# A hybrid decoder step on one core: memory attention with its queries computed by token chunks over all heads, square sums of four heads at once, TensorE's order written by hand, and four output projection tiles placed among the last attention units

## The chip, the core and the metric

The program runs on one core of a Trainium2 chip. The core has TensorE (matmuls into PSUM), VectorE (DVE), ScalarE (ACT), GpSimd (POOL), and SyncE (SP), whose queue issues nearly all of this kernel's transfers. The metric is the device time of one execution in microseconds (us). The kernel before was run three times: median 1817.87 us, from 1817.65 to 1817.94.

## The reference

One layer of a decoder trunk for 1024 prompt tokens and 32 sample tokens (8 sequences of 4), 1056 tokens in all, width 1024, in fp32. Three residual sub-layers follow each other: a mixer (chunked gMLP beside latent attention, then an output projection), a cross-attention into 256 memory tokens, and a gated ConvFFN. The change touches the second:

```python
def mem_attend(h, mk, mv, w_mq, g_mq, w_mo):          # h = rms_norm(x, g_mem_x)
    q = rms_norm((h @ w_mq).reshape(n, t, MEM_HEADS, MEM_HEAD_DIM), g_mq)   # 4 heads of 128
    s = einsum('nthd,nmhd->nhtm', q, mk) * MEM_HEAD_DIM ** -0.5
    p = softmax(s)
    o = einsum('nhtm,nmhd->nthd', p, mv).reshape(n, t, MEM_WIDTH)
    return o @ w_mo
```

The prompt's 1024 tokens share one memory (`mk`, `mv` computed earlier in the same program). Each of the 8 sample sequences has its own cached keys and values of 256 memory tokens, read from DRAM. The result is added to `x`, and the sum goes to the ConvFFN.

## The kernel before

Every fp32 operand of a large matmul is split into a high and a low part of a faster type (`split`, L197: ACT writes the high part, DVE the low part), and a product is three matmuls, high by high, high by low, low by high (`mm3`, L180). Activations lie transposed, features on partitions and tokens along the free axis.

Memory attention (`mem_attention`, L1804) comes behind the mixer's output projection (tile `b`, operands `mx`). Its work is in units of one head `h` and a group `g` of 256 prompt tokens, 16 units in all.

- `query(h, c)` projects head `h` for chunk `c` of three (384, 384 and 288 tokens; the last 32 are the sample tokens): 24 matmuls into PSUM tile `b`. ACT squares the result (`qsq`) and casts it (`qh`), DVE makes `ql`. `tok_sums` (L292) then sums the squares over the 128 features: three matmuls against a column of ones, one column of output each, into tile `st`. After the third chunk DVE works out the head's norm factors `rm` in a chain of small instructions.
- `scores(h, g)`: 12 matmuls into `s` and the softmax (DVE maximum, ACT exponential, DVE division).
- `values(h, g)`: four transposes of the probabilities into `t`, the split into `th` and `tl`, 6 matmuls with the values into `t`, and the split back into `qh`, `ql`.
- The sample part: `sample_scores` and `sample_values` go through the 8 sequences, each with one 512 KB tile of keys or values in `skT` (6 buffers, and once a buffer of `raw`).

Loops before: over heads, in each over the three chunks; the units of head `h - 1` stand between the chunks of head `h`; the units of head 3 and the sample part stand alone behind the last query. The projection with `w_mo` follows (`out`, L2002: per tile 24 matmuls into `y`, 16 tiles for two token halves of 528), then the FFN.

A head's projection weight is brought in by `stream` (L1566): a 512 KB load into `raw` (3 buffers), POOL multiplies it by the gain in place (L1576), ACT casts it to `hi` (L201), DVE makes `lo` (L202). `hi` and `lo` have 3 buffers each. The memory's own keys and values pass through `raw` as well (`memory`, L1822).

What sets the order: the functions write the program, and a list scheduler then orders the instructions of every engine and of the SP queue by its own estimates, unless the code stands under `manual_schedule` for an engine. In this stage nothing did before. Each engine, and SP, then runs its list strictly in that order, and a row waits until all it needs is there, with everything behind it on that engine.

## Time and profile before

| what | us |
|---|---|
| median of three runs | 1817.87 |
| the profiled execution's own time | 1818.09 |
| its span, first to last instruction | 1816.4 |
| TensorE busy in the span | 1794.4 (99%) |
| mean granted TensorE clock | 0.997 of full |
| first query matmul of memory attention | at 981.65 |
| first matmul of the `w_mo` projection | at 1083.02 |
| first matmul of the FFN's block that follows the projection | at 1135.99 |

Times "at" are microseconds from the start of the span. A timeline row gives start, duration, engine, line, operation, tile written and tiles read, shape, and behind it, in brackets, how long the engine had been idle and who released it. The durations of neighbouring matmuls overlap, so the cost of one is the distance from its start to the next start. `st<-ones,qsq` is a sum of squares; `b<-xh,hi` a query matmul; `y<-qh,hi` the projection.

### The profile page before, as it was taken

How to read it: one execution, taken by the hardware profiler on the slowest of the kernel's cores; microseconds unless marked ns; L12 is line 12 of the kernel's file. 1: busy time of each engine (PE TensorE's matmuls, PEld its weight loads, DVE VectorE, ACT ScalarE, POOL GpSimd, SP SyncE). 2: the span in 40 equal slices, each digit the busy share in tenths (PEclk: the TensorE clock that was granted, in tenths of full speed). 3: DMA queues.
4: the chain of work that ended last, by engine and by line, in shares of the span. 5: the costliest groups of instructions: out<-in, count | busy, mean ns of one | idle time of the engine just before them, and what ended most of it. 6: DMA issues, size and time to landing. Idle time of an engine off the chain costs nothing.

```text
span 1816.4 us, 39284 instructions
## 1 busy us (share of the span) xinstructions
PE 1794.4 (99%) x14194; PEld 1702.2 (94%) x14194; DVE 1354.0 (75%) x2796; ACT 918.5 (51%) x1909; POOL 713.5 (39%) x868
## 2 busy tenths in 40 slices
PE   9999999999999999999999999999999999999999
PEld 8999777769999999998899979999999999999999
DVE  7864777657678777787645768998888888878664
ACT  7435676766556565556433557533333333344442
POOL 1021655534455454553023012476667777400000
PEclk9999999999999999999999999999999999999999
DMA  8101354558776666663645156223222222595252
GB/s 325 47 18 67 119 178 128 164 174 233 223 205 188 192 188 181 186 192 124 190 153 190 37 188 213 64 81 94 74 71 73 81 72 93 145 324 163 87 148 78
DMA packets 153188, 261.19 MB, mean 144 GB/s; under 512 B 20897, under 2 KB 97538, under 8 KB 152994
## 3 DMA queue, kind: packets, MB, share of 16 engines
q1 hardware_dynamic: 152130, 257.63, 46.0%
q8 instruction: 112, 1.84, 0.4%
q10 hardware_dynamic: 864, 1.05, 0.2%
q14 instruction: 82, 0.67, 0.1%
HBM read 212.79 MB, written 45.82 MB: 142 GB/s over the span
## 4 chain that ended last, share of the span: by engine, by line
PE 81%; DVE 5%; ACT 1%; issue 1%; POOL 1%; SPq 0%; DMA 0%; DVEq 0%; ACTq 0%; POOLq 0%
PE s L186 22%; PE d L186 12%; PE b L186 8%; PE F L186 7%; PE X L186 7%; PE E L186 7%; PE A L186 3%; PE y L186 3%; PE o L1047 2%; PE o L1538 2%; PE tp L1032 1%; PE tp L186 1%; PE s L1423 1%; PE tp L985 1%; PE t L186 1%
## 5 line engine op out<-in xcount | busy, mean ns | idle before, releaser
L186 PE MATMUL s<-w2h,ch 128*128 128x256 f32 x1018 | 301.8, 297 | 0.0
L186 PE MATMUL s<-w2h,cl 128*128 128x256 f32 x1018 | 293.3, 288 | 0.0
L186 PE MATMUL s<-w2l,ch 128*128 128x256 f32 x1018 | 292.9, 288 | 0.0
L186 PEld LDWEIGHTS s<-w2h,ch 128*128 128x128 f32 x1018 | 191.5, 188 | 3.3 <-issue 2.9
L186 PEld LDWEIGHTS s<-w2h,cl 128*128 128x128 f32 x1018 | 191.3, 188 | 0.4 <-DVE rqa L258 0.4
L186 PEld LDWEIGHTS s<-w2l,ch 128*128 128x128 f32 x1018 | 191.7, 188 | 0.0
L1459 DVE TENSOR_REDUCE ss<-sq 128x16 f32<-128x1024 f32 x128 | 155.3, 1213 | 29.2 <-ACT sq L1456 29.1
L1408 POOL TENSOR_TENSOR cl<-cT,ch 128x512 fp32r<-128x512 f32 x64 | 86.1, 1346 | 196.7 <-ACT ch L1404 184.2
L1456 ACT ACTIVATE sq<-s 128x512 f32<-128x512 f32 x128 | 76.5, 598 | 72.4 <-PE s L186 72.2
L201 ACT CAST a<-brb 128x528 fp32r<-128x528 f32 x77 | 48.8, 634 | 109.3 <-PE d L186 105.9
L1453 ACT ACTIVATE sq<-s 128x512 f32<-128x512 f32 x128 | 76.8, 600 | 49.8 <-PE s L186 38.2
L202 DVE TENSOR_TENSOR a<-brb,a 128x528 fp32r<-128x528 f32 x77 | 54.3, 708 | 55.1 <-ACT a L201 55.0
L186 PE MATMUL d<-a,w 128*128 128x264 f32 x768 | 95.2, 284 | 0.0
L186 PEld LDWEIGHTS d<-a,w 128*128 128x128 f32 x768 | 94.3, 188 | 0.0
L2148 POOL TENSOR_TENSOR lo<-s,hi 128x1024 fp32r<-128x1024 f32 x20 | 63.3, 3164 | 45.9 <-ACT hi L2147 45.9
L186 PE MATMUL mm<-wlo,xh 128*128 128x256 f32 (+3 forms) x272 | 77.0, 286 | 0.1
L2203 ACT COPY a<-A 128x264 f32<-128x264 f32 x43 | 16.1, 376 | 120.6 <-PE A L186 113.2
L186 PE MATMUL mm<-whi,xh 128*128 128x256 f32 (+3 forms) x272 | 77.0, 285 | 0.0
L186 PE MATMUL mm<-whi,xl 128*128 128x256 f32 (+3 forms) x272 | 76.9, 287 | 0.0
L1404 ACT CAST ch<-cT 128x512 fp32r<-128x512 f32 x128 | 73.5, 628 | 0.2 <-issue 0.2
L2269 POOL TENSOR_TENSOR cv<-cv,row 128x1056 f32<-128x1056 f32 x22 | 65.1, 2958 | 21.0 <-ACT cv L2268 21.0
L186 PE MATMUL d<-a,hi 128*128 128x264 f32 x552 | 72.0, 284 | 0.0
(756 smaller groups left out, 6359.3 us busy)
## 6 DMA issues: line engine op xcount, KB each, us to landing
cT<-cT SPq DMA_DIRECT2D x256, 160.0 KB, 2.6
ck<-ck SPq DMA_DIRECT2D x256, 144.0 KB, 3.5
raw<-w_up SPq DMA_DIRECT2D x44, 512.0 KB, 3.6
wsumd<-wsum SPq DMA_DIRECT2D x26, 512.0 KB, 3.9
actd<-cv SPq DMA_DIRECT2D x44, 264.0 KB, 2.3
brb<-actd SPq DMA_DIRECT2D x44, 264.0 KB, 5.9
wsum<-w_down SPq DMA_DIRECT2D x22, 512.0 KB, 3.6
raw<-wsumd SPq DMA_DIRECT2D x20, 512.0 KB, 3.8
```

What stands on the lines that cost most here:

```text
L186: x = self.nc.tensor.matmul(out, l, r, start=first and i == 0, stop=last and i == len(seq) - 1)
L201: first = {"act": nc.scalar.copy, "pool": nc.gpsimd.tensor_copy, "dve": nc.vector.tensor_copy}[eng](hi, src)
L202: low = lambda: nc.vector.tensor_tensor(lo, src, hi, ALU.subtract)
L1047: nc.tensor.matmul(u["o"][g : g + 64, o : o + m * P], s["v"][:, j, h % 4], th[:, z * P : (z + m) * P], start=j == 0, stop=b == len(banks) - 1,
L1404: nc.scalar.copy(d["h"][:, k], src[k])
L1408: (nc.vector if k else nc.gpsimd).tensor_tensor(d["l"][:, k], src[k], d["h"][:, k], ALU.subtract)
L1453: nc.scalar.activation(sq[:, 0], ps[:, :, n0 : n0 + 256], AF.Square)
L1456: nc.scalar.activation(sq[:, 1], pt.rearrange("p (e d) -> p e d", e=2), AF.Square)
L1459: yield lambda: nc.vector.tensor_reduce(s["ss"][:, g0 : g0 + 2].rearrange("p e (z h) -> p z e h", z=2), sq.rearrange("p z e (h d) -> p z e ...
L1538: nc.tensor.matmul(s["o"][j * 32 : j * 32 + 32], S[:, q * 4 + j], d["ck"][:, j, :257], start=q == 0 and j > 0, stop=q == 7)
L2148: eng.tensor_tensor(lo, src, hi, ALU.subtract)
L2269: nc.gpsimd.tensor_tensor(cv, cv, row, ALU.mult)
```

## The change

Queries now run by token chunk, and inside a chunk over the four heads: `query(h, c)` with four chunks of 256, 256, 256 and 288 tokens, 16 calls of 24 matmuls. All four projection weights are thus used in the first four calls and again in each later chunk; the fourth weight has buffers of its own (`wx`), the others keep the three of `hi` and `lo` until the last chunk.

The sums of squares of the four heads of a chunk are made together: `square_sums(c)` multiplies a block of 32 columns of ones with each head's 256 or 288 squares, one head per 32 output partitions, ACT copies the result (`rows`), and `roots(c)` transposes it (two transposes, three for the last chunk) so that tokens come to lie on partitions; one DVE chain then serves four heads.

TensorE's order is written by hand as 23 slots: in slot `s` stand the scores of unit `s - 5`, the query of number `s`, the values of unit `s - 7` and the transposes of unit `s - 6`. The slots from 16 on have no query; the sample part and four projection tiles (`ahead`, first token half, output columns of `j` = 0 and 1) stand there. Those four tiles take their PSUM from the query's `b`, their residual from early loads, and their result lies in the room of FFN operands that are written later (`room`). `out` does the other twelve. `skT` has 5 buffers now and no tile in `raw`; the sample keys' first five loads are written in the program behind slot 7. The other engines and the SP queue are still ordered by the scheduler.

```diff
-    def stream(self, src, kt, g=None, eng="act", tag="", raw=None):
+    def stream(self, src, kt, g=None, eng="act", tag="", raw=None, hl=None):
 
         nc = self.nc
         p, pr = (self.wd, self.wd) if tag else (self.wp, self.wr)
         if raw is None:
             raw = self.t(pr, [P, 8, P], F32, "raw" + tag)[:, :kt]
             nc.sync.dma_start(raw, src)
-        hi, lo = (self.t(p, [P, 8, P], FR, x + tag)[:, :kt] for x in ("hi", "lo"))
+        hi, lo = hl or (self.t(p, [P, 8, P], FR, x + tag)[:, :kt] for x in ("hi", "lo"))
...
-        roots = self.t(pp, [P, 512], F32, "sx", 1)
+        bank = lambda tag, n: self.t(pp, [P, 512], F32, tag, n)
+        for tag in "bst":
+            bank(tag, 2)
...
+        wx = [self.t(p, [P, 8, P], FR, f"wx{n}") for n in "hl"]
...
-        w, st = {}, {}
+        w, qsq, pr, ts = {}, {}, {}, {}
 
         def query(h, c):
-            o, n = CH[c]
-            if c == 0:
-                st[h] = self.t(pp, [P, 512], F32, "st", 1)
-            ps = self.t(pp, [P, 512], F32, "b", 2)[:, :n]
+            o, n = 256 * c, 288 if c == 3 else 256
+            ps = bank("b", 2)[:, :n]
             self.mm3(ps, [(w[h][0][:, k], w[h][1][:, k]) for k in range(8)], [(xh[:, k, o : o + n], xl[:, k, o : o + n]) for k in range(8)])
-            sq = self.t(p, [P, 384], F32, "qsq", 2)
-            nc.scalar.activation(sq[:, :n], ps, AF.Square)
-            self.pad(sq, c)
+            qsq[h] = self.t(p, [P, 288], F32, f"qsq{h}", 1)[:, :n]
+            nc.scalar.activation(qsq[h], ps, AF.Square)
             self.split(qh[:, h, o : o + n], ql[:, h, o : o + n], ps, gmq)
-            self.tok_sums(st[h], sq, c, self.ones)
-            if c < 2:
-                return
-            nc.vector.tensor_scalar(qs[:, h], ps[:, 256:], gmq, None, ALU.mult)
-
-            r = rm[:, h]
-            nc.vector.tensor_tensor(r, st[h][:, :9], r3, ALU.mult)
-            nc.vector.tensor_tensor(r, r, r3, ALU.mult)
-            self.rsqrt(p, r, r, 1.0 / 128)
-            nc.vector.tensor_tensor(r, r, r3, ALU.mult)
-
-        pr = {}
-
-        def scores(h, g):
-            ps = self.t(pp, [P, 512], F32, "s", 2).rearrange("p (e n) -> p e n", e=2)
+            if c == 3:
+                nc.vector.tensor_scalar(qs[:, h], ps[:, 256:], gmq, None, ALU.mult)
+                nc.gpsimd.tensor_tensor(qm[h], blk, qs[:, h].unsqueeze(1).broadcast_to([P, NB, NS]), ALU.mult)
...
+        rows = self.t(p, [P, 384], F32, "rows", 1)
+
+        def square_sums(c):
+
+            n = 288 if c == 3 else 256
+            st = bank("st", 1)[:, :n]
+            for h in range(4):
+                nc.tensor.matmul(st[32 * h : 32 * h + 32], self.ones[:, :32], qsq[h], start=True, stop=True)
+            if c == 3:
+                nc.gpsimd.memset(rows[:, n:], 1.0)
+            nc.scalar.copy(rows[:, :n], st)
+
+        def roots(c):
+
+            m, t = 3 if c == 3 else 2, slice(2 * c, 9 if c == 3 else 2 * c + 2)
+            st = bank("st", 1)[:, : m * P].rearrange("p (k n) -> p k n", k=m)
+            for k in range(m):
+                nc.tensor.transpose(st[:, k], rows[:, k * P : k * P + P], self.ident)
+            x = self.t(p, [P, 3, 4], F32, "rsq", 2)[:, :m]
+            r = rt[:, t].unsqueeze(2).broadcast_to([P, m, 4])
+            nc.vector.tensor_tensor(x, st.rearrange("p k (h e) -> p k h e", h=4)[:, :, :, 0], r, ALU.mult)
+            nc.vector.tensor_tensor(x, x, r, ALU.mult)
+            xf = x.rearrange("p k h -> p (k h)")
+            self.rsqrt(p, xf, xf, 1.0 / 128)
+            nc.vector.tensor_tensor(rm[:, t], x, r, ALU.mult)
...
+        units = [(h, g) for g in range(4) for h in range(4)]
+
+        def scores(i):
...
+        def trans(i):
+            src = pr.pop(i)
+            tp = bank("t", 2).rearrange("p (k n) -> p k n", k=2)
             for k in range(2):
                 for e in range(2):
                     nc.tensor.transpose(tp[:, k, e * P : e * P + P], src[:, e, k * P : k * P + P], self.ident)
-            th, tl = (self.t(p, [P, 2, 256], FR, x, 2) for x in ("th", "tl"))
-            self.split(th, tl, tp)
+            ts[i] = [self.t(p, [P, 2, 256], FR, x, 1) for x in ("th", "tl")]
+            self.split(*ts[i], tp)
+
+        def values(i):
+            h, g = units[i]
...
+                    skv.append(self.t(ps_, [P, 4, 256], F32, "skT", 5))
...
+        def sample_scores(b0, b1):
+            if b0 == 0:
+                sample["s"] = bank("sx", 1)[:, :256]
+            for b in range(b0, b1):
                 kT = skv.pop(0)
                 for h in range(4):
-                    nc.tensor.matmul(sample["s"][heads[h]], sample["q", h][:, b], kT[:, h], start=b == 0, stop=b == NB - 1)
-                if b != 6:
-                    sample_load(1)
-            if z:
-                sample["p"] = self.t(ps_, [P, 1, 256], F32, "pf")
-                self.softmax(ps_, sample["p"], sample["s"].unsqueeze(1), P, sample["sc"])
-
-        def sample_values():
-            tp = self.t(pp, [P, 512], F32, "st", 1)[:, :256].rearrange("p (k n) -> p k n", k=2)
+                    nc.tensor.matmul(sample["s"][heads[h]], qm[h][:, b], kT[:, h], start=b == 0, stop=b == NB - 1)
+                sample_load(1)
...
+        def sample_trans():
...
+                if b < 4:
+                    f()
+                else:
+                    sample["m", b] = f
...
+                if b0 == 0:
+                    sample_load(1)
+                    sample["m", b + 4]()
...
-        for h in range(4):
-            w[h] = self.stream(I["w_mq"][h], 8, "g_mem_x")
-            if h == 2:
-                sample_load(6)
+        def project(h):
+            hl = None if h < 3 else wx
+            w[h] = self.stream(I["w_mq"][h], 8, "g_mem_x", hl=hl)
+
+        def slot(s):
+            c, h = divmod(s, 4)
+            if s >= 5:
+                scores(s - 5)
+            query(h, c)
+            if c and h == 0:
+                roots(c - 1)
+            if s >= 7:
+                values(s - 7)
+            if s >= 6:
+                trans(s - 6)
             if h == 3:
-                sample_load(1, self.t(self.wr, [P, 8, P], F32, "raw").rearrange("p k n -> p (k n)").rearrange("p (h n) -> p h n", h=4))
-            for c in range(3):
-                query(h, c)
-                if h == 0 and c == 0:
-                    self.token_roots(p, roots, r3, 2)
+                square_sums(c)
...
+        with tc.manual_schedule(engines={E.PE}):
+            for s in range(16):
+                if s < 4:
+                    project(s)
+                slot(s)
+                if s == 0:
+                    self.token_roots(p, bank("sx", 1), r3, 2)
+                    nc.vector.tensor_copy(rt, r3)
                     memory()
+                if s == 7:
+                    sample_load(5)
+            self.close("x")
+            px = self.open("xo1", side="right")
+            flat = lambda x: x.bitcast(F32).rearrange("p k n -> p (k n)").rearrange("p (j n) -> p j n", j=2)
+            room = [flat(self.t(px, [P, 4, QT], FR, f"{n}1{q}")) for n in self.FORMS[:3] for q in "hl"]
+            y0 = [room[:2], room[2:4]]
...
+            early = {(j, e): residual(pe, 0, 4 * e + j) for j in range(2) for e in range(2)}
+            wo = [weight(j) for j in range(3)]
+
+            def ahead(j, e):
+
+                res = early[j, e]
+                for c in range(2):
+                    t = slice(c * QT, c * QT + QT)
+                    ps = bank("b", 2)[:, :QT]
+                    self.mm3(ps, [(wo[j][0][:, 4 * e + k], wo[j][1][:, 4 * e + k]) for k in range(4)], [(qh[:, k, t], ql[:, k, t]) for k in range(4)])
+                    nc.vector.tensor_tensor(res[:, t], ps, res[:, t], ALU.add)
+                leave(pe, 0, j, e, res, y0[0])
+
+            for s in range(16, 23):
+                if s < 21:
+                    scores(s - 5)
+                if s < 19:
+                    sample_scores(3 * (s - 16), min(3 * (s - 15), NB))
+                elif s < 22:
+                    ahead(*divmod(s - 19, 2))
+                if s == 16:
+                    roots(3)
+                if s == 19:
+                    sample_trans()
+                if s > 20:
+                    sample_values(4 * (s - 21))
+                if s == 22:
+                    ahead(1, 1)
+                values(s - 7)
+                if s < 22:
+                    trans(s - 6)
+            sample_out()
...
-        for j in range(4):
-            if j == 3:
-                w[j] = weight(j)
-            out(0, j, w[j], y1[j // 2])
-            if j % 2:
-                self.operands(y1[j // 2], j // 2, ops[0], self.FORMS)
-        w[0] = weight(0)
+        self.operands(y0[0], 0, ops[0], self.FORMS)
+        wo.append(weight(3))
+        for j in (2, 3):
+            out(0, j, wo[j], y0[1])
+        self.operands(y0[1], 1, ops[0], self.FORMS)
+        for n in self.FORMS[:3]:
+            form(self.pools["xo1"][1], 1, n)
+        wo[0] = weight(0)
```

How the orders move, at three places. The names are those of the code with a number for each tile; `w_mq` is the DRAM weight of the query projection, `mkT` the sample keys, `blk` a small constant, `w_mo` the projection weight behind.

The SP queue around the start of the stage, before:

```order
L1572 DMA raw_15998<-w_mq 128x1024
...
L1572 DMA raw_16262<-w_mq 128x1024
L1769 DMA res_73<-res_15745 128x288
L1818 DMA blk_15844<-c_blkT 128x256
L1897 DMA skT_16269<-mkT 128x1024
...
L1897 DMA skT_16279<-mkT 128x1024
L1572 DMA raw_16538<-w_mq 128x1024
L1897 DMA raw_16545<-mkT 128x1024
L1884 DMA raw_16859<-w_mo 128x512 x2
```

and now:

```order
L1572 DMA raw_15924<-w_mq 128x1024
...
L1572 DMA raw_15960<-w_mq 128x1024
L1769 DMA res_73<-res_15745 128x288
L1821 DMA blk_15849<-c_blkT 128x256
L1922 DMA skT_16258<-mkT 128x1024
...
L1922 DMA skT_16266<-mkT 128x1024
L1572 DMA raw_15996<-w_mq 128x1024
L1909 DMA raw_16874<-w_mo 128x512 x2
```

The rows shown are the loads of the second, third and fourth head's weight. The queue is the same up to `blk`; between the third and the fourth weight stand five sample loads where six stood (the first and the last of them are shown).

TensorE from the first query on, before (one row of each group: `b` with 384 or 288 columns is a query chunk, `hi_15850` the first head's weight, `hi_16000` the second's, `hi_16264` the third's):

```order
L186 MATMUL b_15856<-xh_14871,hi_15850 128x384
L186 MATMUL b_15914<-xh_14871,hi_15850 128x384
L296 MATMUL st_15855<-ones_61,qsq_15881 128x1 x3
L186 MATMUL b_15946<-xh_14871,hi_15850 128x288
L186 MATMUL b_16006<-xh_14871,hi_16000 128x384
L186 MATMUL b_16055<-xh_14871,hi_16000 128x384
L186 MATMUL b_16122<-xh_14871,hi_16000 128x288
L186 MATMUL b_16282<-xh_14871,hi_16264 128x384
```

and now (`wxh` is the fourth head's weight):

```order
L186 MATMUL b_15867<-xh_14871,hi_15862 128x256
L296 MATMUL sx_15896<-ones_61,acc_2202_14874 128x1 x3
L186 MATMUL b_15931<-xh_14871,hi_15926 128x256
L186 MATMUL b_15967<-xh_14871,hi_15962 128x256
L186 MATMUL b_16001<-xh_14871,wxh_15844 128x256
L1854 MATMUL st_16030<-qsq_2334_15892,ones_61 32x256
L1854 MATMUL st_16030<-qsq_2354_16026,ones_61 32x256
L186 MATMUL b_16036<-xh_14871,hi_15862 128x256
L1864 MATMUL st_16065<-ident_60,rows_15857 128x128 x2
L186 MATMUL s_16087<-kh_15840,qh_15838 128x256
```

The third weight was read first by the seventh group of a query, it is now read by the third; the fourth weight stands right behind it, and no unit stands between.

TensorE at the end of the stage, now (`sx<-skT,pm` are sample values, `b<-qh,hi` a projection tile, `t<-th,vh` the values and `t<-ident,pr` the transposes of a unit):

```order
L186 MATMUL b_17236<-qh_15838,hi_16884 128x264
L1966 MATMUL sx_17269<-skT_16993,pm_17138 32x128 x8
L1966 MATMUL sx_17269<-skT_17046,pm_17144 32x128 x8
L186 MATMUL t_17312<-th_17232,vh_15842 128x256
L1889 MATMUL t_17321<-ident_60,pr_17175 128x128 x4
L1966 MATMUL sx_17269<-skT_17052,pm_17146 32x128 x8
L1966 MATMUL sx_17269<-skT_17300,pm_17149 32x128 x8
L186 MATMUL b_17364<-qh_15838,hi_16884 128x264
L186 MATMUL t_17397<-th_17326,vh_15842 128x256
L186 MATMUL y_17474<-qh_15838,hi_16891 128x264
```

The last four sample values stand behind the first four with one unit's values and one unit's transposes between; projection tiles stand ahead of and behind the two groups, where before all of them came after the last unit.

148 lines of the change are left out of this document (69 added, 79 removed).

## The prediction

> **What bounds the kernel now.** I read the page first, then busy times by stretch, then single rows where the change acts.
>
> ```profile
> span 1816.4 us, 39284 instructions
> PE 1794.4 (99%) x14194; PEld 1702.2 (94%) x14194; DVE 1354.0 (75%) x2796; ACT 918.5 (51%) x1909; POOL 713.5 (39%) x868
> ```
>
> TensorE sets the time: a gain must be fewer TensorE cycles or fewer of its waits. The stretches of this stage (busy time of each engine, granted clock, share and rate of the DMA engines):
>
> ```profile
> 981.65:1050.00 68.35, 68.35 (x485) 68.35 (x485) 44.82 (x158) 33.15 (x82) 8.61 (x13) 1.00 0.29 102
> 1062.00:1085.00 23.00, 20.40 (x234) 16.10 (x233) 15.19 (x37) 12.37 (x35) 5.79 (x8) 1.00 0.71 247
> 990.00:992.00 2.00, 2.00 (x17) 2.00 (x16) 1.94 (x5) 1.66 (x4) 0.18 (x1) 1.00 1.02 420
> ```
>
> While queries run, TensorE never idles; behind them it idles 2.6 us of 23. The third row shows what the loads reach when the queue is full, 420 GB/s, or 1.25 us for a 512 KB tile.
>
> Prices, by distance from start to start. Eight neighbouring rows of the TensorE timeline:
>
> ```profile
> 990.56 0.34 PE L186 MATMUL b<-xh,lo 128*128 128x384 f32 x1
> 990.73 0.72 PE L296 MATMUL st<-ones,qsq 128*128 128x1 f32 x6
> 991.32 0.36 PE L186 MATMUL s<-kh,qh 128*128 128x256 f32 x1
> 991.52 0.29 PE L186 MATMUL s<-kl,qh 128*128 128x256 f32 x1
> 991.64 0.28 PE L186 MATMUL s<-kh,qh 128*128 128x256 f32 x1
> 991.76 0.28 PE L186 MATMUL s<-kl,qh 128*128 128x256 f32 x1
> 991.88 0.29 PE L186 MATMUL b<-xh,hi 128*128 128x288 f32 x1
> 992.01 0.29 PE L186 MATMUL b<-xl,hi 128*128 128x288 f32 x1
> ```
>
> A matmul of 384 columns costs 0.174, of 288 columns 0.132, of 256 columns 0.12. One sum of squares costs 0.59, and the matmul behind it starts its neighbour 0.08 late (0.20 for 0.12): 0.67 in all. From the chain of waits (start, time, work):
>
> ```profile
> 1009.98 0.50 PE t L1868 x4
> 1054.79 2.37 PE sx L1910 x40
> 1069.87 0.57 PE sx L1935 x16
> 1083.18 29.38 PE y L186 x243
> 1124.96 1.03 PE q L2034 x16
> ```
>
> Four transposes take 0.50 at most, a sample score 0.059, a sample value 0.036, a projection matmul 0.121 (a tile of 24: 2.9). The last row is the nearest to the new sums of squares: 32 columns of ones against 264 columns, four groups beside each other.
>
> **The change part by part.**
>
> *TensorE work.* Queries: before 8 x 24 x 0.174 + 4 x 24 x 0.132 = 46.1; now 12 x 24 x 0.12 + 4 x 24 x 0.132 = 47.2: plus 1.1. Twelve sums of squares go: minus 8.0. Four `square_sums` come, each half of the 1.03 row, plus 0.08: plus 2.4 (bounds: 2.1 without the late start, 4.2 if the four heads did not run beside each other but cost 0.12 for each of 8 passes). Nine transposes at 0.125: plus 1.1. Sum: minus 3.4. The four moved tiles cost the same in either place.
>
> *Waits that went with the old order.* From 981.65 to the first projection matmul at 1083.02 pass 101.4 us. Priced work: queries 46.1, sums 12 x 0.67 and the first token sums 0.67 = 8.7, scores and values 32 x 0.72 = 23, transposes with the late start behind them 16 x 0.45 = 7.2, sample scores 64 passes 3.8, sample values 128 passes 4.6, three sample transposes 0.9, some twelve late starts elsewhere 1.0: 95.3. So 6.1 us are waits, 2.7 as idle time and the rest hidden in durations. Four tiles of 2.9 us, standing between the last units, can cover all of it: minus 6.1. Together minus 9.5 at best.
>
> *What is late now.* Weights. Before, the third and the fourth were first read here:
>
> ```profile
> 1011.29 0.34 PE L186 MATMUL b<-xh,hi 128*128 128x384 f32 x1
> 1031.84 0.34 PE L186 MATMUL b<-xh,hi 128*128 128x384 f32 x1
> ```
>
> Now, without waits, the first query ends at 984.6, the token sums at 985.2, the second query at 988.1, and there the third weight is needed; the fourth at 991.0. When they come, the SP queue, POOL, ACT and DVE of the profile tell, whose lists the change leaves alike up to there:
>
> ```profile
> 979.68 0.33 SPq L1572 DMA_DIRECT2D raw<-w_mq  x1
> 981.45 2.77 SPq L1818 DMA_DIRECT2D blk<-c_blkT  x1
> 984.27 3.22 SPq L1897 DMA_DIRECT2D skT<-mkT  x6
> 987.59 0.54 SPq L1572 DMA_DIRECT2D raw<-w_mq  x1
> 986.19 2.57 POOL L1576 TENSOR_TENSOR raw<-raw,cols 128x1024 f32<-128x1024 f32 x1 [3.38 <-DMA raw<-w_mq]
> 998.11 1.90 POOL L1576 TENSOR_TENSOR raw<-raw,cols 128x1024 f32<-128x1024 f32 x1 [6.35 <-DMA raw<-mkT]
> 988.79 1.05 ACT L201 CAST hi<-raw 128x1024 fp32r<-128x1024 f32 x1 [5.04 <-POOL raw L1576]
> 989.87 1.23 DVE L202 TENSOR_TENSOR lo<-raw,hi 128x1024 fp32r<-128x1024 f32 x1 [2.80 <-ACT hi L201]
> 991.08 0.61 DVE L208 SCALAR_TENSOR_TENSOR ql<-b,gmq,qh 128x384 fp32r<-128x384 f32 x1
> ```
>
> Third weight: issued at 979.68, multiplied by 988.76, cast by 989.84, `lo` by 991.1. Behind it on DVE, now as before, stands the first query's `ql`, which frees one of the two `b` banks; it takes about 0.5 for 256 columns, so the third query starts at about 991.6: a wait of 3.5, ending at 994.5.
>
> Fourth weight. Loads in this queue land one behind the other; issue to landing of the third weight, of the sixth sample tile and of the fourth weight, from the DMA view of their stretches:
>
> ```profile
> raw<-w_mq SPq DMA_DIRECT2D x1, 512.0 KB, 6.4
> skT<-mkT SPq DMA_DIRECT2D x1, 512.0 KB, 9.9
> raw<-w_mq SPq DMA_DIRECT2D x1, 512.0 KB, 10.4
> ```
>
> The fourth weight takes the sixth place, behind five sample tiles: issue at about 987.0, landing at about 997.0. POOL 1.9, ACT 1.05, DVE 1.23, each with a short handover: `lo` at about 1001.2. The query can do two matmuls without it; it ends at about 1003.9 and not at 997.4: 6.5 more. (Bounds: with 6.4 to landing 3.0, with 10.4 it is 7.0. I take the sixth tile's, since it has the same bytes ahead.) The square sums of chunk 0 stand right behind this query and wait for ACT's last square: 0.6. Sum of the front: plus 10.6. Nothing covers it, since TensorE's order is fixed and the first scores stand two queries further on.
>
> *First softmax.* The factors of chunk 0 are one DVE chain behind `roots(0)`; DVE's list sets the maximum of the second unit ahead of the chain's last step. The second scores end 4.4 us behind the roots (0.8 + 2.9 + 0.7), the factors and maxima are done at about 6.0; exponentials and division by
>
> ```profile
> L2131 ACT ACTIVATE pr<-s,nm,rm 128x256 f32<-128x256 f32 x18 | 10.1, 570 | 2.7 <-DVE rm L1848 2.7
> L2131 ACT ACTIVATION_READ_ACCUMULATOR pr<-s,nm,rm 128x1 f32 x18 | 3.7, 205 | 0.0
> L2136 DVE TENSOR_SCALAR pr<-pr,rsum 128x256 f32<-128x256 f32 x19 | 7.4, 431 | 0.1
> ```
>
> are 2 x 0.78 + 0.16 + 2 x 0.43 = 2.6, so the first transposes can start at 8.6; TensorE is there at 7.3. Plus 1.3 (0 if DVE is ahead of my count). In the slots behind it ACT and DVE have some 3.2 us of work each in 4.8: no wait.
>
> *The end.* SP issues four residual loads and three weight sums, 1.8 MB or 4.4 us at 420 GB/s, behind the last query and ahead of the sixth sample key, which comes about 0.4 late and the seventh and eighth as much: 0.8. Unit 12's division stands on DVE behind the sample maximum: 0.5. The sixth to eighth sample values are asked for only when the first three are read:
>
> ```profile
> DMA to landing us min/median/max: 3.6/6.8/10.8
> ```
>
> (the sample tiles). With the shortest time, 3.6, and 1.25 for each further tile the eighth lands some 6.9 us behind the start of `sample_values(0)` and is needed after 5.4: with the two handovers 1.9. Plus 3.2, between 0 and 6 (one more load time of 2 to 3 us where writes stand ahead in the queue).
>
> *The clock.* Waits of 3.5 and 6.5 us have not occurred in this stage. What short activity does elsewhere in the program:
>
> ```profile
> 211.50:214.95 3.45, 2.07 (x10) 1.36 (x10) 2.08 (x5) 1.75 (x4) 1.03 (x2) 1.00 0.43 116
> 214.95:218.40 3.45, 3.45 (x12) 2.83 (x10) 2.46 (x9) 0.00 (x0) 0.26 (x1) 0.50 0.71 239
> 218.40:221.80 3.40, 3.40 (x16) 2.45 (x15) 1.56 (x6) 0.88 (x2) 3.06 (x5) 0.50 0.50 154
> ```
>
> One stretch of 3.4 us with TensorE 60% busy is followed by two with half the clock. A wait of 6.5 us empties such a stretch, so I expect one to two at half speed behind it: a loss of 1.7 to 3.4, I take 2.5; 0 if it does not happen. After the first wait the half clock costs nothing, as the fourth weight is later anyway. By the Trainium skill ("TensorE: Matmul & The Clock Gate", Part 1) the clock halves after an idle window of about 3.4 us and comes back after one busy window; by that rule the loss would be 1.7 and the sum 0.8 lower. That 60% sufficed here speaks for the row.
>
> *Sum*, against the profiled execution's 1818.1: minus 9.5, plus 10.6 + 1.3 + 3.2 + 2.5 = 17.6: plus 8.1, 1826.2; the median lies 0.2 lower: **1826**.
>
> **The rivals.**
> - *The order pays.* The third and fourth weight do not hold TensorE. For it: the loads could share bandwidth rather than queue. Against: the third weight's own rows leave 3.5 whatever the fourth does. It decides if `lo` of the third weight is there by 988.1 and of the fourth by 991.0, 3 and 10 us sooner than the rows have it. Without front and clock: 1818.1 - 9.5 + 4.5 = 1813, faster. 5%.
> - *The front only.* The waits for weights come as forecast, but the clock holds and the end is covered by the moved tiles: 1818.1 - 9.5 + 10.6 + 1 = 1820, no measurable change. For it, a stretch of this stage that was 76% busy and followed by full clock:
>
> ```profile
> 1078.50:1081.90 3.40, 2.57 (x24) 1.60 (x16) 1.88 (x5) 1.83 (x5) 0.00 (x0) 1.00 0.90 285
> ```
>
> Against: 6.5 us idle is another case. 17%.
> - *The last loads decide.* SP stands at a projection tile's write or an FFN load when the sixth sample value is asked for, and the three land with the median 6.8: 3.2 more for the first and as much shift for the others, beside a second half clock of 1.7: 1831. It decides once the queue is held more than 2 us. 13%.
> - *The forecast*, 1822 to 1829: 65%.
>
> **How the numbers follow.** No change means within 0.2% of 1817.9, 1814.2 to 1821.5; a measurement of this kernel tells about that much. Faster: 6% (the first rival and some of the unknown). No change: 16%. Slower: 78% (forecast, third rival). The range, 1819.5 to 1830.5, leaves out the first rival and the end of the third.
>
> **What would show it.** TensorE idle at L186 `b` of the third query, released by DVE, about 3.5, and of the fourth, about 6, released by `wxh` and `wxl`; the fourth weight landing about 10 behind its issue; a granted clock below 1 in the 7 us behind. `st` sums at about 0.5 for a group of four heads. From the ninth slot to the sixteenth no idle TensorE; at the end waits of `sx` for `skT`. The first projection matmul in `y` at about 1102 where 1094.6 would be equal (1083.0 plus four tiles). Wrong if the third query starts before 990, if the fourth weight lands before 994, or if the tail's waits are not mostly gone.

## The result, and the profile after

The changed kernel takes 1834.7 us (median of six runs, 1827.0 to 1835.7) against 1817.9 for the kernel before: a ratio of 1.0083, with a 95% interval of 1.0066 to 1.0100. It is slower by 16.8 us where 8.1 were forecast, and outside the forecast range (1819.5 to 1830.5). The profiled execution took 1834.8.

The page, span and busy times:

```profile
span 1833.0 us, 39420 instructions
PE 1795.4 (98%) x14259; PEld 1702.0 (93%) x14259; DVE 1353.7 (74%) x2805; ACT 919.8 (50%) x1921; POOL 713.2 (39%) x865
```

TensorE is busy 1.0 longer than before (with what half clock stretches in it), in a span 16.6 longer: the rest is waiting. Busy times by stretch, after: from the first query to the last matmul of the last query, from there to the first projection matmul in `y`, and from there to the first matmul in `X`, where the FFN begins (start and end, length, busy time of TensorE, its weight loads, DVE, ACT and POOL, granted clock, share and rate of the DMA engines):

```profile
982.95:1063.26 80.31, 72.23 (x569) 68.75 (x570) 51.25 (x167) 38.48 (x100) 6.67 (x7) 0.94 0.23 84
1063.26:1108.82 45.56, 38.05 (x411) 32.44 (x410) 26.07 (x75) 19.50 (x51) 10.23 (x15) 0.93 0.69 244
1108.82:1152.23 43.41, 41.84 (x358) 40.02 (x356) 36.84 (x54) 32.96 (x58) 6.98 (x6) 1.00 0.55 172
```

From the first query to the first `y` pass 125.9 us; before it was 101.4, and with the four moved tiles (11.6) 113.0: plus 12.9. The third stretch, without those tiles, was 41.3 before: plus 2.1. The first query starts 1.3 later. Outside these stretches the two profiles agree (676.6 from `X` to the last matmul in both).

Where TensorE waits from 980 to 1160, from the list of its waits (us in total, times, longest); before, no entry of this list was above 0.7:

```profile
PE b L186 <- ACT wxh L201: 5.6, 1, 5.6
PE sx L1930 <- DMA skT<-mkT: 3.2, 1, 3.2
PE sx L1966 <- DMA skT<-mv: 2.8, 2, 2.5
PE b L186 <- DVE ql L208: 1.6, 1, 1.6
PE X L186 <- DVE row L2154: 1.6, 1, 1.6
PE sx L1966 <- POOL pm L1949: 1.5, 1, 1.5
PE b L186 <- DVE rqx L247: 0.5, 1, 0.5
PE b L186 <- DVE wxl L202: 0.5, 1, 0.5
PE t L1889 <- DVE pr L2216: 0.3, 1, 0.3
```

The third query (1.6) and the fourth (5.6 and 0.5) wait for their weights. At the end come the sixth sample key (3.2), the factors `pm` (1.5) and the last sample values (2.8), and, named nowhere in the forecast, `X` for DVE's `row`. The clock around the first long wait, window by window:

```profile
993.14:996.55 3.41, 1.04 (x9) 0.83 (x8) 0.48 (x1) 0.75 (x2) 0.00 (x0) 1.00 0.95 365
996.55:999.96 3.41, 0.23 (x1) 0.23 (x2) 0.25 (x1) 1.04 (x1) 1.89 (x1) 0.50 0.24 89
999.96:1003.38 3.42, 2.96 (x13) 2.66 (x14) 0.98 (x1) 0.00 (x0) 0.00 (x0) 0.50 0.37 116
1003.38:1006.79 3.41, 3.41 (x20) 2.76 (x20) 0.00 (x0) 0.70 (x2) 0.00 (x0) 0.50 0.10 37
```

Three windows run at half clock, the first of them nearly idle anyway. Two more follow the waits at the end, at 1075 and 1102.

### The profile page after: what moved, and what is told of

It reads as the page before. It is cut to its first block, busy times and chain, and to the rows that moved or that the text cites. A ratio compares the mean times of both kernels' runs of the same rounds, so it can differ in the third digit from the quotient of the medians.

```text
span 1833.0 us, 39420 instructions
## 1 busy us (share of the span) xinstructions
PE 1795.4 (98%) x14259; PEld 1702.0 (93%) x14259; DVE 1353.7 (74%) x2805; ACT 919.8 (50%) x1921; POOL 713.2 (39%) x865
## 4 chain that ended last, share of the span: by engine, by line
PE 80%; DVE 4%; ACT 2%; DMA 2%; issue 1%; SPq 0%; POOL 0%; DVEq 0%; ACTq 0%; POOLq 0%
PE s L186 22%; PE d L186 12%; PE b L186 8%; PE F L186 7%; PE X L186 7%; PE E L186 7%; PE A L186 3%; PE y L186 2%; PE o L1047 2%; PE o L1538 2%; PE tp L1032 1%; PE tp L186 1%; PE s L1423 1%; PE b L1606 1%; PE tp L985 1%
```

## The experiments

"Saves" and "costs" below are medians against the changed kernel's 1834.7. The medians of the kernel before, taken beside the experiments on the same chip, lie between 1817.6 and 1818.9; each ratio is against the one beside it. Single executions of one kernel lie up to 10.5 us apart (run 6), and in the seventeen profiles the first query of this stage starts between 979.9 and 986.2, though no edit is meant to act ahead of it. So a saving is read from medians, and where it arises from distances inside the stage. The intervals of runs 3, 13 and 14 overlap with that of the changed kernel: their savings of about 4 us are likely, not certain.

The code is shortened: `...` marks rows left out, and comments are added for the reader.

**1. The fourth weight ahead of the sample keys in SP's queue.** Each of the five loads is put behind it:

```
+            self.raw_dma = nc.sync.dma_start(raw, src)
...
+                    if b < 5:
+                        self.behind(x, self.raw_dma)
```

> The changed kernel with one thing edited: SP issues the load of the fourth query weight ahead of the five early sample keys, which now stand behind it; buffers as before. Theory (the weight's place in SP's queue makes the fourth query wait): it is still issued at about 988.2, where the raw buffer comes free, lands some 3.7 later (992) instead of 8.3, and the query starts 3.1 behind the landing, as in the changed kernel: at about 995.1, a wait of 1 to 1.5 instead of 5.6 (4.4 less). A window of the clock is then no longer empty, so the half clock at 996.6 goes as well: 3.5 less. 1834.7 - 4.4 - 3.5 = 1826.8. Rival (the transfers share the bandwidth, so the order of issue decides little): landing at 8 behind issue, 1834.

1827.5, ratio 1.0048 (1.0035 to 1.0062): 7.2 saved. From the timeline, the load's issue and the fourth query:

```profile
991.03 0.33 SPq L1572 DMA_DIRECT2D raw<-w_mq  x1
998.17 0.39 PE L186 MATMUL b<-xh,wxh 128*128 128x256 f32 x1 [1.24 <-ACT wxh L201]
```

and POOL's start on the weight, in this run and (below) in the changed kernel, where the load was issued at 988.25:

```profile
995.14 1.90 POOL L1576 TENSOR_TENSOR raw<-raw,cols 128x1024 f32<-128x1024 f32 x1 [6.10 <-DVE rqa L259]
```

```profile
996.71 1.89 POOL L1576 TENSOR_TENSOR raw<-raw,cols 128x1024 f32<-128x1024 f32 x1 [10.63 <-DMA raw<-w_mo]
```

POOL starts on it 4.1 behind the issue instead of 8.5 (the brackets do not name its landing, which the DMA view has for the changed kernel alone, 8.3), and the wait falls to 1.2 and 0.8. So most of the fourth wait is the load's place behind the keys. One half-speed window is left in the front. The profiled execution, 1833.4, was the longest of five.

**2. The same weight in a free sample tile,** so that it needs no raw buffer and is issued some 6 us earlier:

```
+                    if b < 5:
+                        self.behind(x, self.w3_dma)
...
+            if h == 3:
+                raw = self.t(ps_, [P, 4, 256], F32, "skT", 5)   # ..., seen as [P, 8, P]
+                self.w3_dma = nc.sync.dma_start(raw, I["w_mq"][h])
```

> The changed kernel with the fourth query weight loaded into one of the five sample tiles, which is free, and issued ahead of the early sample keys; the weight waits for no raw buffer any more. Theory: issued at about 982.6, landing before 988, POOL, ACT and DVE have it ready by about 991.5, before the fourth query's place at 994.2. The wait of 5.6 and the one of 0.5 behind it go, and the half clock (3.5): 1834.7 - 9.6 = 1825. The wait of 1.6 ahead of the third query stays. Rival (POOL, ACT and DVE are late rather than the load): the query still waits 2 us or more, 1829 to 1832.

1825.9, ratio 1.0040 (1.0026 to 1.0054): 8.8 saved, and no half clock in the front. The raw buffer, which DVE's `kl` held until 988.2 in the changed kernel, was the rest of the load's delay; 1.0 is left ahead of the fourth query, for DVE's `ql`. SP's issue, and POOL's start on the weight:

```profile
980.52 0.41 SPq L1988 DMA_DIRECT2D skT<-w_mq  x1
988.28 2.02 POOL L1576 TENSOR_TENSOR skT<-skT,cols 128x1024 f32<-128x1024 f32 x1 [4.23 <-DMA skT<-w_mq]
```

POOL waited for the transfer until 7.8 after its issue, though little stood ahead of it; run 9 takes that up.

**3. TensorE kept at work in the fourth wait:**

```
+            if s == 3:
+                idle = bank("s", 2)[:, :256]
+                for i in range(40):
+                    nc.tensor.matmul(idle, xh[:, i % 8, :P], xh[:, i % 8, :256], start=True, stop=True)
```

> The changed kernel with 40 matmuls of 128x256 added on TensorE ahead of the fourth query, into a free bank that nobody reads: 4.8 us at 0.12 each, inside the wait of 5.6. They do no work for the result. Theory (the wait halves the clock behind it, and that costs time of its own): the query starts at 999.7 as before, but the three half-speed windows from 996.6 to 1006.8 are gone and the fifth query starts some 3.5 earlier: 1834.7 - 3.5 = 1831.2. Rival (the half clock costs nothing, since other engines set the pace there): 1834.7. Other rival (the clock falls whatever stands there): half clock at the same place, 1834.7 or more.

1830.7, ratio 1.0070 (1.0056 to 1.0083): 4.0 saved by work that nobody needs. The added work and the fourth query behind it:

```profile
991.56 4.85 PE L1992 MATMUL s<-xh 128*128 128x256 f32 x40
996.85 0.39 PE L186 MATMUL b<-xh,wxh 128*128 128x256 f32 x1 [0.44 <-ACT wxh L201]
```

and two stretches of the front, with the granted clock in the third column from the end:

```profile
993.60:997.10 3.50, 3.06 (x27) 2.86 (x25) 0.27 (x1) 1.05 (x1) 1.90 (x1) 1.00 0.27 99
997.10:1000.50 3.40, 2.64 (x22) 2.44 (x22) 0.96 (x1) 0.00 (x0) 0.00 (x0) 1.00 0.36 118
```

The clock stays full, and from the first query to the fifth pass 21.5 us instead of 24.2. Of these 2.7 us, 0.4 are not the clock's: the weight landed after 7.9 instead of 8.3, and the fourth query came that much sooner. From the fourth query to the fifth pass 5.2 us instead of 7.5, so the half clock in the front is worth 2.3.

**4. The loads of the last part:** residual tiles and weight sums behind the sixth to eighth key, own tiles for the last three values, all eight `pm` at once.

```
-            early = {(j, e): residual(pe, 0, 4 * e + j) for j in range(2) for e in range(2)}
...
+                    if s == 16:   # behind sample_scores(0, 3), and behind key 8 in SP's queue
+                        early.update({(j, e): residual(pe, 0, 4 * e + j) for j in range(2) for e in range(2)})
...
-                pm = self.t(pe, [P, 2, 4, NS], F32, "pm", 4)
+                pm = self.t(pe, [P, 2, 4, NS], F32, "pm", 8)
```

> The changed kernel with the loads of its last part moved and given room: the four early residual tiles and the weight sums stand behind the sixth to eighth sample keys in SP's queue; the last three sample values have tiles of their own and are asked for with the first five; all eight masked factors (pm) are made at once, ahead of the projection's adds on POOL. Theory (the waits at the end are places in queues): the waits of 3.2 (sample key 6), 1.5 (pm) and 2.8 (last values) go, and with them the two half-speed windows at 1075 and 1102, some 1.7 each: 1834.7 - 10.9 = 1823.8. Rival (the waits only change place: the residual tiles are late for the projection tiles, or the key waits for its buffer): 1830 or more, with a wait at L186 b<-qh or at the sample keys.

1826.7, ratio 1.0047 (1.0034 to 1.0061): 8.0 saved. The part from the last query to the first `y` is 36.5 long instead of 45.6: 9.1 less, where the theory had 10.9. 3 us of that come back where `X` starts:

```profile
1139.81 0.39 PE L186 MATMUL X<-b210h,hi 128*128 128x264 f32 x1 [2.26 <-DVE row L2161]
```

```profile
1141.20:1148.00 6.80, 6.80 (x34) 6.77 (x34) 5.16 (x10) 3.34 (x7) 0.33 (x2) 0.50 0.01 3
```

The wait ahead of `X` (timeline), grown to 2.3, is followed by 6.8 us at half clock (busy times by stretch).

**5. DVE's order in the front,** on top of run 2: `kl` and `vl` behind the weights' low parts.

```
+                if s == 3:
+                    self.behind(self.low, second)   # second: the second query's low part
+                    for f in late:
+                        self.behind(f(), self.low)
...
+                    self.lows = []
                     memory()
+                    late, self.lows = self.lows, None
```

> The kernel of the weight loaded into a sample tile, with the order on DVE edited too: the low parts of the memory's keys and values (kl, vl, 1.2 each) stand behind those of the third and fourth weight and behind the low part of the second query. Theory (the 1.6 ahead of the third query, and 1.0 in front of the fourth there, are places in DVE's list): both waits go, 1825.9 - 2.6 = 1823.3. Rival (POOL's fold and ACT's cast are what is late, DVE's order matters little): a wait of 1 or more stays at the third query, 1825 to 1826.

1827.9, ratio 1.0053 (1.0039 to 1.0066): nothing gained over run 2. ACT had taken over the delay:

```profile
992.31 1.05 ACT L201 CAST wxh<-skT 128x1024 fp32r<-128x1024 f32 x1 [4.82 <-POOL skT L1576]
993.27 0.38 ACT L1841 ACTIVATE qsq<-b 128x256 f32<-128x256 f32 x1
994.58 0.39 PE L186 MATMUL b<-xh,wxh 128*128 128x256 f32 x1 [1.24 <-DVE ql L208]
```

In ACT's list the fourth weight's cast stood ahead of the second query's square; it waited 4.8 for POOL, and the query's bank stayed taken. The rival (POOL and ACT are late) is nearer, but it was an order, not a load on the engines.

**6. One more y tile drawn.** `for _ in range(2): self.t(pp, [P, 2, 512], F32, "y", 3)` in place of one such line.

> The changed kernel with one unused y tile more drawn at the start of the projection, so that the tiles behind it take the next of the three y bank pairs, as before the change. Theory (the wait of 1.6 ahead of the first X product comes from the bank: four tiles fewer of y move the last product a into the bank pair on which X opens, and X then waits for DVE's read of it, row L2154): the wait goes, 1834.7 - 1.6 = 1833.1. Rival (X waits for its operands or the casts behind the projection): 1834.7, with the same idle time ahead of X.

1834.1, ratio 1.0078 (1.0058 to 1.0097), with the wait of 1.6 in place. It tells nothing of the bank: a tile that nothing uses is dropped when the program is built, and in the traces TensorE, DVE, ACT and POOL do the same instructions in the same order as in the changed kernel. So it is a second measurement of that kernel: the median is 0.6 lower, the single executions lie between 1826.8 and 1837.3. Runs 11 and 15 put the question properly.

**7. The four moved tiles behind the last unit.**

```
-                elif s < 22:
-                    ahead(*divmod(s - 19, 2))
...
-                if s == 22:
-                    ahead(1, 1)
...
+            for j in range(2):   # behind sample_out()
+                for e in range(2):
+                    ahead(j, e)
```

> The changed kernel with the four moved projection tiles behind the last unit and the sample part instead of among the last units; all else stays. Theory (the tiles cover the softmax of the last units, the term of 6.1): the waits come back, some 1.3 in each of the slots 20 to 23 and for the sample factors pm: 4 to 6 more, 1839.7. Rival (the covered waits were small, or the tiles are themselves what puts loads and POOL adds in the way): no change or faster, 1831 to 1835.

1841.7, ratio 1.0125 (1.0108 to 1.0142): 7.0 dearer. New among the waits are these:

```profile
PE st L1942 <- DVE pf L2215: 2.5, 1, 2.5
PE y L186 <- DVE res L2057: 1.9, 1, 1.9
PE t L186 <- DVE tl L202: 0.9, 1, 0.9
```

So the tiles do cover waits. The first and the third row, 3.4 us, stand among the last units. The 7.0 hold more than that: the 1.9 ahead of `y` comes from the tiles' new place, and from the last query on four windows run at half clock instead of two. The size of the cover, 6.1 in the forecast, is not measured by itself.

**8. All edits so far** (2, 4, 5, 6, sample scores dealt 3, 2, 3).

> All edits together: weight in a sample tile, DVE's order of the front, the loads and tiles of the last part, the y bank, and the eight sample scores dealt 3, 2 and 3 to the slots instead of 3, 3 and 2. Theory (the loss is the sum of these waits and of the half clock behind them, and the order itself pays): 1834.7 - 8.8 (weight) - 2.6 (DVE) - 8.0 (last part) - 1.6 to 2.3 (bank) - 1 (sample keys) = 1812 to 1813, faster than before by 0.3%. Rival (waits only move on, the order itself pays nothing): 1818 or more.

1823.4, ratio 1.0031 (1.0022 to 1.0041): 10 to 11 above the theory. Some waits had moved on: ACT's of run 5, `X`'s with 6.8 us at half clock behind it, and one at unit 12, of which DVE's rows tell the cause:

```profile
1068.10 0.17 DVE L1871 TENSOR_TENSOR rm<-rsq,rt 128x12 f32<-128x12 f32 x1
1069.50 0.42 DVE L2230 TENSOR_REDUCE nm<-sx 128x1 f32<-128x256 f32 x1 [1.23 <-PE sx L1940]
1069.84 0.22 DVE L2231 TENSOR_TENSOR nm<-nm,rm 128x2 f32<-128x2 f32 x2
1071.96 1.09 PE L1889 MATMUL t<-ident,pr 128*128 128x128 f32 x4 [1.61 <-DVE pr L2238]
```

Unit 12's factors were there at 1068.3. Its product `nm` stood behind the maximum of the sample scores, which waited for a key; its transposes then waited 1.6.

**9. The block mask behind the fourth weight,** on top of run 2.

```
-        nc.sync.dma_start(blk, I["c_blkT"].partition_broadcast(P))
...
+                    x = nc.sync.dma_start(blk, I["c_blkT"].partition_broadcast(P))   # ahead of sample_load(5)
+                    self.behind(x, self.w3_dma)
```

> The kernel with the fourth weight in a sample tile, and one more edit: the load of the block mask (blk, 128 KB, one row to all partitions) stands behind that weight in SP's queue instead of ahead of it. In the kernel without this edit the weight took 7.7 from issue to landing, though nothing but the third weight and blk stood ahead. Theory (blk's transfer holds the queue): landing after 3.7 to 4.5, POOL's fold some 3 us sooner, the wait ahead of the fourth query (1.0) gone: 1825. Rival (the sample keys issued right behind share the bandwidth, whatever stands ahead): landing at 7 or more still, 1825.9.

The weight's landing in the DMA view, and from the timeline POOL's fold and DVE beside it:

```profile
skT<-w_mq SPq DMA_DIRECT2D x1, 512.0 KB, 5.6
```

```profile
989.83 1.98 POOL L1576 TENSOR_TENSOR skT<-skT,cols 128x1024 f32<-128x1024 f32 x1 [2.05 <-DMA skT<-w_mq]
989.97 1.87 DVE L248 TENSOR_SCALAR rqy<-rqx 128x3 int32<-128x3 int32 x1
991.75 1.21 DVE L202 TENSOR_TENSOR vl<-raw,vh 128x1024 fp32r<-128x1024 f32 x1
```

5.6 lies between the two. POOL starts on the weight 6.0 behind its issue, not 7.8: `blk` ahead of it cost 1.8. The remaining 1.9 above run 1's 4.1 do not fit the rival, the loads right behind it: in run 1 five sample keys were issued 0.4 behind the weight as well. What run 1 did not have is a load still under way ahead of it; here the third weight was issued 1.8 ahead. No run takes that apart. The kernel takes 1829.1, ratio 1.0058 (1.0042 to 1.0073), some 3 more than in run 2 in spite of the earlier landing: POOL's fold now began while DVE still had `vl` and the third weight's low part ahead of it, and a DVE instruction on 128x3 elements (0.16 in the changed kernel) took 1.87 beside that fold. The third query waited 3.4 instead of 1.6.

**10. The front's lists in the order of need,** on top of 5 and 9: ACT's cast of the weight behind the second query's, the token roots behind the third query.

```
+                    self.behind(self.cast, qcast)   # qcast: the second query's cast
...
-                if s == 0:
+                if s == 2:
                     self.token_roots(p, bank("sx", 1), r3, 2)
```

> The front with all of its queues in the order in which TensorE needs the results: weight in a sample tile and blk behind it; on DVE the low part of the third weight, the low parts of the first two queries, that of the fourth weight, then kl and vl; on ACT the second query's square and cast ahead of the fourth weight's cast (in the kernel with DVE's order alone ACT held them behind that cast, which waited 4.7 for POOL); the token roots behind the third query. Theory (the rest of the front's waits, 1.6 and 1.0, are places in DVE's and ACT's lists): TensorE goes from the first query to the fifth without a wait of over 0.3; 1834.7 - 8.8 - 2.6 = 1823. Rival (the engines are full there, a wait moved comes out elsewhere): 1825 or more.

In the front only 0.6 of `wxl` is left, and from the first query to the last pass 70.3 us (72.4 in run 2, 80.3 in the changed kernel). The median is 1825.9, ratio 1.0050 (1.0036 to 1.0065), no better than run 2, with runs from 1823.6 to 1831.0. The profiled execution was the 1823.6, with a granted clock of 0.997; the others had 0.993 or 0.994. Where they lost the clock is not on record.

**11. The FFN's banks.**

```
         pp = self.open("psf", space=PSUM)
+        for tag in "AX":
+            self.t(pp, [P, 512], F32, tag, 2)
```

> The changed kernel with the banks of the FFN's first pool dealt in another order: A takes the first two banks and X the two behind them. The unused y tile of the run on the bank was taken out by the compiler, so that that run could not tell. Theory (X opens on the bank pair that DVE's read of the product a holds, L2154): the wait of 1.6 ahead of the first X product goes, 1833.1. Rival (the wait is for work that X needs, not for the bank): the wait stays, 1834.7.

The wait ahead of `X` is gone, so it was the bank. Later in the FFN, where `d` opens, a new one stands:

```profile
PE d L186 <- DVE G L2362: 1.1, 1, 1.1
```

1833.5, ratio 1.0086 (1.0072 to 1.0099): 1.2 saved, within the uncertainty.

**12. All edits once more,** with the front of run 10, the banks of run 11, the late values behind the keys, and in the softmax:

```
+        if n == 1:                       # the sample part
+            self.behind(x, self.nm)      # its maximum behind unit 13's product nm
```

> All edits together: the front in order, the loads and tiles of the last part, the three late sample values behind the keys, the maximum of the sample scores behind unit 13's on DVE (in the first kernel with all edits unit 12's factors stood 1.5 behind it), and the FFN's banks. Theory (waits and the half clock behind them are the whole loss): of the 1823.4 of that kernel go 2.7 of waits in the front, 1.5 of unit 12, 2.3 ahead of X, and four half-speed windows (3.4, 3.4 and 6.8 long, half of it lost): 1823.4 - 2.7 - 1.5 - 2.3 - 6.8 = 1810, below before by 0.4%. Rival (a further wait takes the place of each): 1818 or more.

1814.8, ratio 0.9979 (0.9970 to 0.9988): faster than before, though the theory had 1810.

**13. The first edit of run 4 alone,** residual tiles and weight sums behind the keys.

> One of the three edits of the last part alone: in the changed kernel the four early residual tiles and the weight sums stand behind the sixth to eighth sample keys in SP's queue; the values' tiles and POOL's order stay. Theory (half of what the last part lost is the sixth key's place in the queue): the wait of 3.2 and the half-speed window behind it (1.7) go, 1834.7 - 4.9 = 1829.8, and the waits for pm and for the last values stay. Rival (the gain of 8 with all three edits came from the values and pm): 1833 to 1835.

1831.2, ratio 1.0064 (1.0048 to 1.0079): 3.5 saved. The key's wait falls to 0.4. In the profiled execution, the longest of four (1835.6), the last values wait 4.1 and are followed by 6.8 us of half clock, so part of the gain is handed on there.

**14. TensorE kept at work in the sixth key's wait:** 24 matmuls `kh`, `qh` into a free bank.

> The changed kernel with 24 matmuls of 128x256 added on TensorE ahead of the sixth sample key's scores, into a bank that nobody reads: 2.9 us at 0.12, inside the wait of 3.2. They do no work for the result. Theory (the half clock behind that wait costs time of its own): the wait's end stays, the half-speed window at 1075 is gone, and the part from the last query to the first y product is 1.7 shorter (45.6 to 43.9); the median 1833. Rival (that window comes from the 1.6 to 2 us of little work in front, or costs nothing): the part stays at 45.6 and the window is there.

1831.1, ratio 1.0068 (1.0052 to 1.0083): 3.6 saved. The key's scores begin at 1071.24 and the first moved tile at 1076.83, 5.6 later; in the changed kernel 7.5 later. That window at half clock costs 1.9. The part from the last query to the first `y` is 1.2 shorter, 44.4, since the last values wait 4.1 and 6.8 us at half clock follow them.

**15. All edits, with the bank mended at its origin:** one projection tile takes two of the three `y` bank pairs, and `A` and `X` stay as they were.

```
+                    two_y = c == 1 and (h, j, e) == (0, 2, 0)
...
+                    if two_y:
+                        nc.vector.tensor_tensor(x[:, 0], ps[:, 0], x[:, 0], ALU.add)
+                        ps = self.t(pp, [P, 2, 512], F32, "y", 3)[:, :, :QT]
```

> The last kernel with all edits, with the bank mended in another way: instead of A ahead of X in the FFN's pool, the first projection tile behind the sample part takes two of the three y bank pairs, one per half of its tokens, and adds them in two steps, so that the product a takes the next pair. Theory (the turn of the y bank pairs put a on X's banks; A ahead of X moved the wait of 1.1 to the first product d of the FFN's second half): no wait ahead of X, none ahead of d, 1814.8 - 1.4 = 1813.4. Rival (X waits whichever pair a takes): 1.6 to 2.3 ahead of X again and a half-speed window behind it, 1817 to 1820.

1813.0, ratio 0.9969 (0.9957 to 0.9981): 5.6 us faster than the kernel before. The gain over run 12, 1.8, is not clear, since the single times overlap. Its waits from the first query into the FFN, and its two stretches from the first query to the first `y`:

```profile
PE t L1888 <- DVE pr L2252: 1.0, 2, 0.7
PE b L186 <- DVE rqx L247: 0.5, 1, 0.5
PE sx L1941 <- DMA skT<-mkT: 0.4, 1, 0.4
PE A L2215 <- ACT a L2321: 0.4, 1, 0.4
PE y L186 <- DVE ql L202: 0.3, 1, 0.3
```

```profile
981.74:1051.28 69.54, 69.08 (x569) 66.32 (x570) 51.52 (x167) 38.50 (x100) 6.63 (x7) 1.00 0.29 96
1051.28:1086.97 35.69, 34.56 (x412) 30.18 (x410) 25.33 (x75) 19.45 (x51) 9.79 (x15) 1.00 0.85 313
```

Neither `X` nor `d` waits, as the theory has it: the turn of the `y` bank pairs was the cause. With four tiles fewer the product `a` fell on the pair on which `X` opens.

## Why the prediction was right or wrong

Slower was right; the size was half of what came. Run 15 does the same work in nearly the same order without most of the waits, and serves as a ruler (its profiled execution was the shortest of six, 1811.3): from the first query to the fifth, to the last, to the first `y` it takes 13.5, 56.1 and 35.7 us, the changed kernel 24.2, 56.1 and 45.6.

- **TensorE work and old waits, -9.5: right.** 105.2 us from the first query to the first `y` against 113.0, with 1.7 of waits still in it: -9.4 without them. How much of it is the tiles' cover, put at 6.1, run 7 does not tell by itself.
- **The front, +10.6: right in place, 2.1 too large.** The excess over run 15 is 10.8, of which 2.3 is the clock (run 3); 8.5 is left, 7.7 of it listed waits. The third weight waited 1.6, not 3.5: `blk` was issued in 0.43 instead of 2.77, and the weight landed after 3.6 instead of 6.4; why, no run shows. Its high part was there at 987.1, and DVE did `kl` and `vl` until 989.4 ahead of its low part: the 1.6 that are left are largely DVE's order (run 5). The fourth waited 6.1 in all against 6.5. It was issued at 988.2, not 987.0, because its raw buffer was taken until then, which the working did not ask for; it landed after 8.3, not 9.9. That loads "land one behind the other" holds in so far as loads issued behind a weight did not slow it (run 1); the price of what stands ahead is open in part (run 9).
- **First softmax, +1.3: too large.** 0.35, the bound "DVE is ahead of my count"; slots five to sixteen are as long as in run 15.
- **The end, +3.2: the step that failed.** It cost 9.9, of which 7.4 are waits and the rest mostly clock. The step is the price of the loads ahead of the sixth key: by their bytes they were to make it 0.4 late. They did not put off its issue at all. SP issued it 0.77 behind the first sample score, in the changed kernel as in run 13, where these loads stand behind the keys. They slowed its transfer. In the changed kernel (issue of the sixth to eighth key, then the sixth key's scores):

```profile
1066.95 1.37 SPq L1922 DMA_DIRECT2D skT<-mkT  x3
1074.19 0.64 PE L1930 MATMUL sx<-skT,qm 128*32 128x256 f32 x8 [3.16 <-DMA skT<-mkT]
```

  and its landing in run 13:

```profile
skT<-mkT SPq DMA_DIRECT2D x1, 512.0 KB, 3.6
```

  It is read 7.2 behind its issue, as soon as it is there, instead of landing after 3.6: a wait of 3.2 instead of 0.4. The last values were issued within 1 us of the first value's matmul, but the seventh and eighth were read 7.1 and 7.8 behind their issue, where the working had them land after 4.9 and 6.1: 2.8 of waits against 1.9. The 1.5 for `pm`, behind the projection's adds on POOL, was not seen. My bounds reached 6. The third rival (1831) came nearest in time, and its slow landing of the last values came true; its condition, SP held for more than 2 us, did not, and it did not name the key.
- **The clock, +2.5: right behind the fourth weight (2.3), missing at the end.** The same rule was applied to one wait only. A wait of 3.2 at the key and of 2.5 at the values each cost a window more; run 14 measures 1.9 for the first.
- **The bank of `X`, not in the sum: 1.6.** The working priced the moved tiles at "the same in either place" and did not follow the turn of their banks.

With the measured sizes: -9.4 for the order, 1.7 for run 15's own waits, 10.8 front and clock, 9.9 end and clock, 2.1 in the stretch ahead of `X`, 1.3 ahead of the first query (0.5 of it a wait there, the rest above this stage): 16.4, against 16.6 between the two spans.

## What to carry to other kernels

A new order of the work is worth what its loads and lists allow: for each moved consumer ask when its load is issued, which buffer that load waits for, what stands ahead of it in the queue, and what stands ahead of its helpers on each in-order engine; here the order was worth 9 us and lost some 23 to such places, half clock included. Price a wait together with the clock behind it, and look at the clock even for waits of 2 to 3 us. When tiles are taken out of a rotating pool, follow which bank the next stage opens on.

## What the runs showed of the hardware

**The clock falls after a half-busy window, not only after an idle one.** In all seventeen profiles the clock changes on a grid of 3.41 us. Counted from the matmul records, from 20 us after the start on: of 26 windows at full clock in which TensorE was busy less than 40%, all were followed by one at half clock; between 40% and 60% it was 28 of 56; between 60% and 80%, 8 of 131; between 80% and 99%, none of 528 (and 10 of 8115 fully busy ones, all at one place far ahead of this stage). A window that itself runs at half clock ended the half clock in 1 case of 21 when busy less than 90%, and in 71 of 85 above. So where a wait falls on the grid decides whether it costs a second time. That fits the spread of the runs, 8.7 us in the changed kernel and 3.8 in the six of run 15, but was not followed up in each. By the Trainium skill ("TensorE: Matmul & The Clock Gate", Part 1) the window of 3413 ns runs free and half clock follows at least one idle window; the grid agrees with the measured 3.41, the condition does not: 1.04 of 3.41 us busy sufficed at 993.14 above, and 1.39 of 3.41 around the first matmul of `X` in run 4, in the last window before the 6.8 us:

```profile
1137.79:1141.20 3.41, 1.39 (x11) 1.39 (x12) 3.41 (x7) 3.41 (x8) 0.10 (x1) 1.00 0.66 204
```

**A small load can hold a large one.** 128 KB of `blk`, one row to all partitions, ahead of a weight of 512 KB held it for 1.8 us (run 9), though at the 420 GB/s of the forecast its bytes are worth 0.3. In the three profiles with `blk` ahead (runs 2, 5, 8) POOL starts on the weight 7.8 to 7.9 behind its issue, in the four with `blk` behind it (9, 10, 12, 15) 5.8 to 6.9.

**POOL's work can hold DVE.** Wherever POOL's fold of 128x1024 (1.9) ran in the front while DVE had work on few elements in SBUF, one such instruction began beside it and ended with it: 1.86 at 984.11 in the changed kernel, 1.87 in run 9, where 0.16 is the usual time. DVE's `ql`, which reads `b` from PSUM, kept its 0.48 beside the fold (runs 10, 12, 15):

```profile
984.02 1.94 POOL L1576 TENSOR_TENSOR raw<-raw,cols 128x1024 f32<-128x1024 f32 x1 [0.57 <-DVE rqa L258]
984.11 1.86 DVE L256 SCALAR_TENSOR_TENSOR rqa<-rqy 128x3 f32<-128x3 f32 x1
986.28 0.16 DVE L256 SCALAR_TENSOR_TENSOR rqa<-rqy 128x3 f32<-128x3 f32 x1
```

The Trainium skill ("SBUF — State Buffer", "Who interferes with whom") has such a rule: certain DVE instructions and GpSimd share a pair of ports, which one of them holds for a whole instruction. The rows agree, and the forecast of the front had not used it.
